# One core, a weight stream split on arrival: moving the release of weights behind each projection's evacuation, one stage per projection in gated attention, and a layer-norm row and the last output block moved

## The chip, the cores and the metric

The kernel runs on one core of a Trainium2 chip. The metric is the time of one execution in device microseconds (us). Engines go by the profile's names: PE is TensorE (PEld its weight load), DVE is VectorE, ACT is ScalarE, POOL is GpSimd, SP is SyncE, which here only issues transfers.

## What is computed

256 tokens of width 1024 pass, in fp32, through two layers with adaptive modulation and then a second block. Cut to what matters:

```python
def first_block(x, c, ctx, c_ctx, w_mod, b_mod, ln_g, ln_b, ...):
    for i in range(2):                                   # layer 0: attention, layer 1: pooling
        sh1, sc1, g1, sh2, sc2, g2 = adaln_params(c, w_mod[i], b_mod[i])
        hx = modulate(x, sh1, sc1)                       # x * (1 + sc1) + sh1
        y = latent_diff_attention(...) if i == 0 else multiscale_pool(hx, pool_w, pool_scale)
        x = layer_norm(ALPHA * x + g1 * y, ln_g[i, 0], ln_b[i, 0])
        x = layer_norm(ALPHA * x + g2 * swiglu(modulate(x, sh2, sc2), w_in[i], w_out[i]),
                       ln_g[i, 1], ln_b[i, 1])

def second_block(x, p, ...):
    u = rms_norm(x, norm_mix) @ w_in
    gq, gk, gv, g_lr, g_r, mq, mk, mv, gate_a, gate_b = jnp.split(u, points, axis=-1)
    o_a = gla_chunked(gq, gk, gv, log_sigmoid(g_lr @ gate_w2 + gate_b) / 16)
    y_a = (rms_norm(o_a, gla_out_norm) * silu(g_r)) @ w_branch_a
    y_b = moba_attention(rms_norm(mq), rms_norm(mk), mv) @ w_branch_b
    x = x + (sigmoid(gate_a) * y_a + sigmoid(gate_b) * y_b) @ w_out
    x = x + square(relu(rms_norm(x, norm_mlp) @ w_up)) @ w_down
    return x + sigmoid(rms_norm(x, norm_ple) @ w_ple_gate) * (p @ w_ple)
```

## The kernel before

The 256 tokens are two tiles of 128 (`t` = 0 and 1). Nearly all the work is projections of both tiles with weights that are used once. A weight arrives as raw blocks of 128x1024 fp32 (512 KB) in the order of a fixed plan (class `Stream`), by transfers that SP issues into 11 buffers. Each block is split: ACT writes a rounded copy `hi` (L285), DVE writes the rest `lo` (L291), into 8 pairs of buffers. A product is then three matmuls, hi with the activations' hi, lo with their hi, hi with their lo (L376 to L378 in `mmN`, L390 and L392 in `mmK`, L403 to L405 in `mmK_tail`), so one projection of one token tile to 512 columns is 24 matmuls over four blocks. In between, the plan holds "m" blocks of modulation weights, each one DVE product with a row `crow` (L269), whose sums become the columns `mc`.

The kernel sets the order of every engine's work by hand: each engine runs its instructions in the order in which the program emits them. `st.get(key)` returns a block's hi and lo, and emits splits up to it where they are not there yet. `st.done(keys)` says that blocks are used up, and at each key emits the next split (a hi on ACT and a lo on DVE, with at most one modulation product) as far as 7 pairs ahead:

```python
        def done(self, *keys):
            for key in keys:
                ...
                self.ndone += 1
                self.pump()
```

So the place of `st.done` in the code is the place in the ACT and DVE queues at which three or four splits stand. The buffers that they write come free while PE is still at work on the blocks, in the order in which it reads them.

PSUM tiles come from three tags, `big`, `mm` and `tr`, with two buffers each. A projection's result (`mm`) is evacuated by ACT or DVE, transposes (`tr`) by both: ACT writes the hi half of the transposed activations (`hh`, `xTh`, `obT`, L425), DVE the lo half (`hl`, `xTl`, L426).

Places that the change touches:

- **FFN** (`ffn`): six chunks of hidden columns. For chunk j, `do_g` and `do_u` make gate and up for both tiles, `fin` the product h on DVE (L969), then the output of chunk j-1 (`o(j-1,0)`, `o(j-1,1)`) is interleaved with the transposes of h (`tr(j,t)`, L981 on PE). A table `mid` has functions that run after the up projections of a chunk. In layer 0's FFN, `mid_gb` at chunk 4 makes columns (`Gc`, `Bc`, `g1p`) from modulation sums, and `mid_gbr` at chunk 5 makes three rows of them (`col_row`: two times four transposes on PE at L774, two copies on ACT at L775).
- **Attention's projections** (`proj`, `qk_evac`, `qk_tr`) of the second block: mq, mk, mv, gq, gk, gv, with the scores and values of the MoBA attention as steps between them. `qk_evac` copies a projection (L1280), sums squares (L1284), and normalises (L418 on DVE, POOL, L1287 on DVE). `qk_tr` transposes (L1294) and scales (L1297).
- **Gated attention** (`g_z` to `g_fin`): 16 projections `seq`, and a list `steps` of functions between them, one or two behind each. `g_kv` (L1482, L1489) makes states, `g_o` (L1495, L1500) uses them.
- **ba, bb, up**: the branch projections and the MLP's up projection, with `st.done` ahead of the evacuation; `down`: the MLP's output, in the same pattern as `o`.

Of the kernel before, what the change touches and what calls it, by code (L numbers as in the profile page):

```python
# [18 lines left out]
P = 128  # L19
# [44 lines left out]
UPM = 8  # L64
F32K = (0, 1, 2, 3, 4)
VM = (1, 1, 1, 1, 0, 0, 0, 0)
EN = (0, 2, 0)

FFN_CHUNKS = [(0, 512), (512, 512), (1024, 512), (1536, 256), (1792, 512), (2304, 512)]
U_COLS = dict(gq=(0, 512), gk=(512, 512), gv0=(1024, 512), gv1=(1536, 512), gr0=(2064, 512), gr1=(2576, 512),  # L70
# [101 lines left out]
def body(ctx: ExitStack, tc: tile.TileContext, wst, prm, cst, cst2, poolp, xT_d, cT_d, x_d, head, lam_d,  # L172
# [769 lines left out]
    def ffn(l, fp, x1_ready, after0, mid1, after1, mid):  # L942
        J = len(FFN_CHUNKS)
        ops_ = None
        hT = {}
        hs = {}

        def gu(j, t, which, ps, mid={}):
            c0, w = FFN_CHUNKS[j]
            n = D * w // (P * BW)  # L950
            lh = xlh(t)
            if is32((which, l, j)):
                lh = lambda k: xf[t, k // 4][:, k % 4]
            mmN(ps[:, :w], lh, mkey((which, l, j), n), width=w, mid=mid)

        def do_g(j, t):
            ps = mmt()
            gu(j, t, "G", ps)
            w = FFN_CHUNKS[j][1]
            h = fp.t([P, 512], f"h{t}", bufs=2)  # L960
            A.activation(h[:, :w], ps[:, :w], AF.Silu)  # L961
            hs[j, t] = h

        def do_u(j, t, mid={}):
            ps = mmt()
            gu(j, t, "U", ps, mid)
            w = FFN_CHUNKS[j][1]
            h = hs[j, t]
            V.tensor_tensor(h[:, :w], h[:, :w], ps[:, :w], op=OP.mult)  # L969

        def fin(j, which):
            c0, w = FFN_CHUNKS[j]
            st.done(*mkey((which, l, j), D * w // (P * BW)))

        def tr(j, t):
            w = FFN_CHUNKS[j][1]
            n = w // P
            h = hs.pop((j, t))
            ps = trt()
            for i in range(n):  # L980
                TE.transpose(ps[:, i * P:(i + 1) * P], h[:, i * P:(i + 1) * P], ident)  # L981
            hh = fp.t([P, 4, P], f"hh{t}", F32R, bufs=2)
            hl = fp.t([P, 4, P], f"hl{t}", F32R, bufs=2)
            pv = ps.rearrange("p (k t) -> p k t", t=P)[:, :n]
            split_evac(pv, hh[:, :n], hl[:, :n])
            hT[j, t] = (hh, hl)

        def o(j, t, done):
            n = FFN_CHUNKS[j][1] // P
            hh, hl = hT.pop((j, t))  # L990
            if j == J - 1:
                keys = [("O", l, j, i) for i in range(n)]
                mmK_tail(halves(ops_[t]), [(hh[:, i], hl[:, i]) for i in range(n)], keys)
                if done:
                    st.done(*keys[:HN[l]])
                    st.hold = True
                    st.done(*keys[HN[l]:])
                return
            for i in range(n):
                mmK(halves(ops_[t]), (hh[:, i], hl[:, i]), ("O", l, j, i), j == 0 and i == 0, False)  # L1000
                if done:
                    st.done(("O", l, j, i))

        for j in range(J):
            if j == 0:
                do_g(0, 0)
                do_u(0, 0, {XR[l]: x1_ready})
                if XR[l] == 8:
                    x1_ready()
                do_g(0, 1)  # L1010
                fin(0, "G")
                do_u(0, 1)
                fin(0, "U")
# [12 lines left out]
            if j < J - 1:
                if j > 0:
                    o(j - 1, 0, False)
                tr(j, 0)
                if j > 0:  # L1030
                    o(j - 1, 1, True)
                    tr(j, 1)
            else:
                tr(j, 0)
                o(j - 1, 0, False)
                tr(j, 1)
                o(j, 0, False)
                if l == 0:
                    for b in range(2):
                        st.prescale(("PW", b))  # L1040
                after0(ops_[0])
                if l == 0:
                    st.hold = True
                o(j - 1, 1, True)
                mid1()
                o(j, 1, True)
                after1(ops_[1])
                if l == 1:
                    st.hold = False
                    st.pump()  # L1050
# [38 lines left out]
    def mid_gb():  # L1089
        nx["gb"] = mod_cols(1, 0, 1)  # L1090
        g1p = cp.t([P, 8], "g1p")
        V.tensor_tensor(g1p, mcol(1, 2), prmc("psc"), op=OP.mult)
        nx["g1p"] = g1p

    def mid_gbr():
        nx["G"], nx["B"] = col_row(nx["gb"][0]), col_row(nx["gb"][1])
        cur["grow"] = col_row(nx["g1p"])
        nx["cols"] = mod_cols(1, 1, 2)

    mrs = {}  # L1100
# [165 lines left out]
        a, b = CST2[n]  # L1266
        return c2d[:, a:b] if b <= o_ else c2[:, a - o_:b - o_]

    def proj(c, t, fin, mid={}):
        ps = mmt()  # L1270
        mmN(ps, xlh(t), mkey((c,), 4), mid=mid)
        if fin:
            st.done(*mkey((c,), 4))
        return ps

    qk_wait = []

# [23 lines left out]
    for i, (c, t) in enumerate(seq):  # L1301
        if i == 2 and MQ == 8:
            rx_t(1, prmc("nmix"))
        ps = proj(c, t, t == 1, {MQ: lambda: rx_t(1, prmc("nmix"))} if i == 1 else {})
        qk_evac(c, t, ps)
# [66 lines left out]
    seq = [(c, t) for c in ("mv0", "mv1", "gq", "gk", "gv0", "gv1") for t in range(2)]  # L1372
    per = -(-len(steps) // 9)
    for i, (c, t) in enumerate(seq):
        ps = proj(c, t, t == 1)
        if c[:2] == "mv":
            A.activation(mv[:, t, 512 * int(c[2]):512 * int(c[2]) + 512], ps, AF.Copy)
        elif c == "gq":
            A.activation(gq[:, t], ps, AF.Copy)
        elif c == "gk":  # L1380
            A.activation(gk[:, t], ps, AF.Copy)
        else:
            A.activation(gv[:, t, 512 * int(c[2]):512 * int(c[2]) + 512], ps, AF.Copy)
# [119 lines left out]
    def g_fin(t):  # L1503
# [5 lines left out]
        for h in range(GH):  # L1509
# [4 lines left out]
    tr_evac(s[1], 1, *obT)  # L1514
    seq = [("gb0", 0), ("gb0", 1), ("gb1", 0), ("gb1", 1), ("bb0", 0), ("bb0", 1), ("bb1", 0), ("bb1", 1),
           ("ga0", 0), ("ga0", 1), ("ga1", 0), ("ga1", 1), ("gr0", 0), ("gr1", 0), ("gr0", 1), ("gr1", 1)]
    steps = [lambda: (g_z(0), g_z(1)), lambda: g_b(0), lambda: g_b(1), lambda: (g_kl(0), g_kl(1)), lambda: g_qk(0), lambda: g_qk(1),
             lambda: g_a(0), lambda: g_a(1), lambda: g_kv(0), lambda: g_kv(1), lambda: (g_o(0, 0), g_o(1, 0)), lambda: g_kv(2),
             lambda: (g_o(0, 1), g_o(1, 1)), lambda: g_kv(3), lambda: (g_o(0, 2), g_o(1, 2)),
             lambda: (g_o(0, 3), g_o(1, 3))]  # L1520

    def oblh(t):
        return lambda k: (obT[0][:, k, t * P:(t + 1) * P], obT[1][:, k, t * P:(t + 1) * P])
# [1 line left out]
    for i, (c, t) in enumerate(seq):  # L1525
# [7 lines left out]
        if c[:2] == "bb":  # L1533
            ps = mmt()
            mmN(ps, oblh(t), mkey(("bb", f), 4))
            if t == 1:
                st.done(*mkey(("bb", f), 4))
            V.scalar_tensor_tensor(tb[t][:, sl], tb[t][:, sl], 1.0, ps, op0=OP.add, op1=OP.mult)
        else:
            ps = proj(c, t, t == 1)  # L1540
            if c[:2] == "gb":
                A.activation(tb[t][:, sl], ps, AF.Tanh, scale=0.5)
            elif c[:2] == "ga":
                A.activation(ta[t][:, sl], ps, AF.Tanh, scale=0.5)
            else:
                e = tmp()
                A.activation(e, ps, AF.Tanh, scale=0.5)
                V.scalar_tensor_tensor(gs[t][:, sl], e, 1.0, ps, op0=OP.add, op1=OP.mult)
                V.tensor_tensor(gs[t][:, sl], gs[t][:, sl], gon[:, sl], op=OP.mult)
        for _ in range(1 + (1 < i < 6)):  # L1550
            if steps:
                steps.pop(0)()
        if (c, t) == ("gr1", 0):
            while steps:
                steps.pop(0)()
            g_fin(0)
    g_fin(1)

# [2 lines left out]
    for i, (f, t) in enumerate([(0, 0), (1, 0), (0, 1), (1, 1)]):  # L1561
# [68 lines left out]
    for j in range(1, J):  # L1630
# [139 lines left out]
```

## Time and profile before

| | |
|---|---|
| three runs, us | 1155.54, 1156.95, 1157.97 (median 1156.95) |
| the profiled execution, us | 1158.82 |
| its span on the core, us | 1156.8 (2.0 less than its time) |
| mean granted TensorE clock | 0.993 |
| PE busy | 1116.0 us, 96% of the span, 5186 instructions |
| DVE busy | 760.6 us, 66% |
| ACT busy | 558.8 us, 48% |
| POOL busy | 22.7 us, 2% |
| moved | 234.62 MB, mean 203 GB/s |

Busy shares count matmuls, ALU and activation work, not register or semaphore instructions. The matmuls' ends are modelled and overlap, so time is best read from start to start. A wait is the idle time of an engine in front of an instruction, with what ended it.

### The profile page before, as it was taken

To read this page: it belongs to the slowest core of one execution; us is meant where nothing else is said; L and a number is where in the kernel's file an instruction comes from. 1 tells how busy PE (TensorE), PEld (TensorE's weight loads), DVE (VectorE), ACT (ScalarE), POOL (GpSimd) and SP (SyncE) were. 2 spreads that over 40 slices of the span, in tenths; PEclk is the share of its full clock that TensorE was granted. 3 is DMA by queue.
4 is the path that set the end of the run, shared out by engine and by line. 5 is a ranking of instruction groups with operands and counts; after the bars stand their busy time and mean duration, and the time that the engine had idled before them with its cause. 6 is when DMAs were issued, how large, how long until landed. Compare 5 with 4: busy or idle time off the path is not lost. (4 is left out here: it accounts for less than half of the span.)

```text
span 1156.8 us, 14163 instructions
## 1 busy us (share of the span) xinstructions
PE 1116.0 (96%) x5186; PEld 881.8 (76%) x5186; DVE 760.6 (66%) x1114; ACT 558.8 (48%) x913; POOL 22.7 (2%) x35
## 2 busy tenths in 40 slices
PE   7999888999999999999999999999999999999998
PEld 3578665678888776888887787886777877888887
DVE  7984967669986875677346765455545785555465
ACT  3452456454444527544444755457235374445353
POOL 0000000000000000000000110000000000000000
PEclk9999989999999999999999999999999999999999
DMA  9972742569997915668563755444344645464611
GB/s 360 351 274 102 273 145 66 196 236 357 354 419 286 336 58 203 218 225 300 170 231 119 241 188 180 146 164 153 102 146 130 216 151 195 166 210 163 206 38 37
DMA packets 65922, 234.62 MB, mean 203 GB/s; under 512 B 7323, under 2 KB 8347, under 8 KB 65852
## 3 DMA queue, kind: packets, MB, share of 16 engines
q1 hardware_dynamic: 64080, 227.97, 55.7%
q10 hardware_dynamic: 1772, 5.74, 1.5%
q8 instruction: 41, 0.67, 0.2%
q14 instruction: 29, 0.24, 0.1%
HBM read 232.63 MB, written 1.05 MB: 202 GB/s over the span
## 5 line engine op out<-in xcount | busy, mean ns | idle before, releaser
L291 DVE TENSOR_TENSOR lo<-raw,hi 128x1024 fp32r<-128x1024 f32 x316 | 375.2, 1220 | 139.8 <-ACT hi L285 136.1
L285 ACT ACTIVATE hi<-raw 128x1024 fp32r<-128x1024 f32 x316 | 322.5, 1056 | 82.9 <-PE mm L378 60.9
L376 PE MATMUL mm<-hi,xTh 128*128 128x512 f32 (+1 forms) x872 | 337.6, 387 | 4.0 <-ACT xTh L425 2.7
L377 PE MATMUL mm<-lo,xTh 128*128 128x512 f32 (+1 forms) x872 | 331.8, 380 | 2.0 <-DVE lo L291 1.3
L378 PE MATMUL mm<-hi,xTl 128*128 128x512 f32 (+1 forms) x872 | 332.2, 381 | 0.6 <-DVE xTl L738 0.4
L376 PEld LDWEIGHTS mm<-hi,xTh 128*128 128x128 f32 x872 | 164.1, 188 | 40.8 <-issue 4.7
L378 PEld LDWEIGHTS mm<-hi,xTl 128*128 128x128 f32 x872 | 164.0, 188 | 34.0 <-DVE xTl L426 1.9
L377 PEld LDWEIGHTS mm<-lo,xTh 128*128 128x128 f32 x872 | 164.2, 188 | 33.5 <-DVE lo L291 3.6
L269 DVE SCALAR_TENSOR_TENSOR raw<-raw,crow 128x1024 f32<-128x1024 f32 x80 | 96.7, 1218 | 0.0
L390 PE MATMUL big<-hi,hh 128*128 128x512 f32 x256 | 80.6, 396 | 0.0
L390 PE MATMUL big<-lo,hh 128*128 128x512 f32 x256 | 79.2, 391 | 0.0
L392 PE MATMUL big<-hi,hl 128*128 128x512 f32 x256 | 79.0, 390 | 0.0
L425 ACT ACTIVATE hh<-tr 128x512 fp32r<-128x512 f32 (+1 forms) x40 | 23.0, 576 | 97.4 <-PE tr L981 54.8
L961 ACT ACTIVATE h<-mm 128x512 f32<-128x512 f32 (+1 forms) x24 | 13.5, 561 | 90.2 <-PE mm L378 90.2
L426 DVE TENSOR_TENSOR hl<-tr,hh 128x512 fp32r<-128x512 f32 (+1 forms) x40 | 26.3, 661 | 46.3 <-ACT hh L425 45.6
L392 PEld LDWEIGHTS big<-hi,hl 128*128 128x128 f32 x256 | 48.1, 188 | 10.4
L390 PEld LDWEIGHTS big<-lo,hh 128*128 128x128 f32 x256 | 48.0, 188 | 10.3
L390 PEld LDWEIGHTS big<-hi,hh 128*128 128x128 f32 x256 | 46.7, 188 | 8.6
L420 POOL TENSOR_TENSOR st<-st,half 128x4 f32<-128x4 f32 (+1 forms) x28 | 21.8, 778 | 1036.8 <-DVE st L418 1023.6
L1596 DVE TENSOR_TENSOR h<-h 128x512 f32<-128x512 f32 x16 | 11.0, 688 | 33.6 <-ACT h L1595 33.5
L1595 ACT ACTIVATE h<-mm 128x512 f32<-128x512 f32 x16 | 9.6, 599 | 38.0 <-PE mm L378 38.0
L667 ACT ACTIVATE p<-big,st 128x512 f32<-128x512 f32 x16 | 11.0, 689 | 31.7 <-DVE st L666 31.7
(316 smaller groups left out, 1261.5 us busy)
## 6 DMA issues: line engine op xcount, KB each, us to landing
raw<-in_dram SPq DMA_DIRECT2D x426, 512.0 KB, 5.0
row<-in_dram ACTq DMA_DIRECT2D x8, 512.0 KB, 6.4
tok<-in_dram SPq DMA_DIRECT2D x8, 256.0 KB, 7.5
xa<-in_dram SPq DMA_DIRECT2D x2, 512.0 KB, 5.7
out_dram<-sg SPq DMA_DIRECT2D x3, 256.0 KB, 2.0
pmat<-in_dram ACTq DMA_DIRECT2D x1, 544.0 KB
crow<-in_dram ACTq DMA_DIRECT2D x1, 512.0 KB, 6.8
out_dram<-sg SPq DMA_DIRECT2D x2, 128.0 KB, 1.7
```

What stands on the lines that cost most here:

```text
L269: V.scalar_tensor_tensor(raw, raw, 1.0, crow, op0=OP.mult, op1=OP.mult, accum_out=mc[l][:, nb:nb + 1])
L285: A.activation(hi, raw, AF.Copy)
L291: V.tensor_tensor(lo, raw, hi.bitcast(F32), op=OP.subtract)
L376: TE.matmul(ps, h, hi[:, sl], start=s, stop=False)
L377: TE.matmul(ps, h, lo[:, sl], start=False, stop=False)
L378: TE.matmul(ps, l, hi[:, sl], start=False, stop=e)
L390: TE.matmul(halves[f], h, w[:, f * 512:(f + 1) * 512], start=first and b == 0, stop=False)
L392: TE.matmul(halves[f], l, hi[:, f * 512:(f + 1) * 512], start=False, stop=last)
L420: G.tensor_tensor(r, v, half_e[:, :w], op=OP.pow)
L425: A.activation(dh, ps, AF.Copy)
L426: V.tensor_tensor(dl, ps, dh.bitcast(F32), op=OP.subtract)
L961: A.activation(h[:, :w], ps[:, :w], AF.Silu)
```

## The change

1. `st.done` moves behind the evacuation, in `proj` (which now gets the evacuation as a function), in bb, ba and up. `st.done` is the call that emits the next splits, so these stand behind the evacuation in ACT's and DVE's queues.
2. Gated attention has one entry of `steps` per projection: `g_b` of both tiles together, `g_kl` of both, `g_qk(0)`, `g_qk(1)`, `g_a` of both, `g_kv(0)`, then for each head `g_o` of both tiles and the next head's `g_kv`.
3. In layer 0's FFN the row of `Gc` is made in `mid_gb` (chunk 4) and the row of `g1p` in a new `late_row` behind `tr(4, 1)`; `mid_gbr` at chunk 5 keeps the row of `Bc`.
4. In both FFNs and in the MLP, the split of the last output block is forced by a `st.get` ahead of the second-last output.
5. `EN`, which sets where a layer norm's second tile stands among the last outputs, is 2 in place of 0 in one entry.

```diff
-EN = (0, 2, 0)
+EN = (0, 2, 2)
...
                     o(j - 1, 1, True)
                     tr(j, 1)
+                if (j, 1) in mid:
+                    mid[j, 1]()
             else:
                 tr(j, 0)
+                st.get(("O", l, j, FFN_CHUNKS[j][1] // P - 1))
                 o(j - 1, 0, False)
...
         nx["g1p"] = g1p
+        nx["G"] = col_row(nx["gb"][0])
+
+    def late_row():
+        cur["grow"] = col_row(nx["g1p"])
 
     def mid_gbr():
-        nx["G"], nx["B"] = col_row(nx["gb"][0]), col_row(nx["gb"][1])
-        cur["grow"] = col_row(nx["g1p"])
+        nx["B"] = col_row(nx["gb"][1])
...
-    ffn(0, ..., {XM: mid_xa, 2: mid_g2c, 3: mid_g2r, 4: mid_gb, 5: mid_gbr})
+    ffn(0, ..., {XM: mid_xa, 2: mid_g2c, 3: mid_g2r, 4: mid_gb, (4, 1): late_row, 5: mid_gbr})
...
-    def proj(c, t, fin, mid={}):
+    def proj(c, t, evac, mid={}):
         ps = mmt()
         mmN(ps, xlh(t), mkey((c,), 4), mid=mid)
-        if fin:
+        evac(ps)
+        if t == 1:
             st.done(*mkey((c,), 4))
-        return ps
...
-    steps = [lambda: (g_z(0), g_z(1)), lambda: g_b(0), lambda: g_b(1), lambda: (g_kl(0), g_kl(1)), lambda: g_qk(0), lambda: g_qk(1),
-             lambda: g_a(0), lambda: g_a(1), lambda: g_kv(0), lambda: g_kv(1), lambda: (g_o(0, 0), g_o(1, 0)), lambda: g_kv(2),
-             lambda: (g_o(0, 1), g_o(1, 1)), lambda: g_kv(3), lambda: (g_o(0, 2), g_o(1, 2)),
-             lambda: (g_o(0, 3), g_o(1, 3))]
+    steps = [lambda: (g_z(0), g_z(1)), lambda: (g_b(0), g_b(1)), lambda: (g_kl(0), g_kl(1)), lambda: g_qk(0),
+             lambda: g_qk(1), lambda: (g_a(0), g_a(1)), lambda: g_kv(0)]
+    for h in range(GH):
+        def head(h=h):
+            g_o(0, h)
+            g_o(1, h)
+            if h < GH - 1:
+                g_kv(h + 1)
+        steps.append(head)
...
+            V.scalar_tensor_tensor(tb[t][:, sl], tb[t][:, sl], 1.0, ps, op0=OP.add, op1=OP.mult)
             if t == 1:
                 st.done(*mkey(("bb", f), 4))
-            V.scalar_tensor_tensor(tb[t][:, sl], tb[t][:, sl], 1.0, ps, op0=OP.add, op1=OP.mult)
...
-        for _ in range(1 + (1 < i < 6)):
-            if steps:
-                steps.pop(0)()
+        for f_ in steps[i:i + 1]:
+            f_()
...
             trm(j, 0)
+            st.get(("DN", j, 3))
             down(j - 1, 0, False)
```

**PE in layer 0's FFN, chunk 4, between the up projection of the second tile and the gate projection of chunk 5.** `big` is the FFN's output, `h0` and `h1` the hidden chunk, `Gc` and `g1p` the columns. Before:

```order
L378 MATMUL mm_696_2979<-hi_680_2920,xTl_6_71 128x512
L390 MATMUL big_504_2040<-hi_684_2929,hh0_656_2798 128x512 x2
L390 MATMUL big_504_2040<-lo_685_2931,hh0_656_2798 128x512 x2
L392 MATMUL big_504_2040<-hi_684_2929,hl0_657_2799 128x512 x2
...
L981 MATMUL tr_718_3063<-cst_7_72,h0_677_2891 128x128 x4
L390 MATMUL big_505_2041<-hi_684_2929,hh1_674_2862 128x512 x2
...
L981 MATMUL tr_729_3102<-cst_7_72,h1_679_2918 128x128 x4
L376 MATMUL mm_732_3111<-hi_691_2944,xTh_5_70 128x512
```

After:

```order
L378 MATMUL mm_696_2979<-hi_680_2920,xTl_6_71 128x512
L774 MATMUL tr_719_3052<-cst_7_72,Gc_714_3042 128x128 x4
L774 MATMUL tr_720_3058<-cst_7_72,Gc_714_3042 128x128 x4
L390 MATMUL big_504_2040<-hi_684_2929,hh0_656_2798 128x512 x2
...
L981 MATMUL tr_721_3076<-cst_7_72,h0_677_2891 128x128 x4
L390 MATMUL big_505_2041<-hi_684_2929,hh1_674_2862 128x512 x2
...
L981 MATMUL tr_732_3115<-cst_7_72,h1_679_2918 128x128 x4
L774 MATMUL tr_736_3125<-cst_7_72,g1p_716_3047 128x128 x4
L774 MATMUL tr_737_3131<-cst_7_72,g1p_716_3047 128x128 x4
L376 MATMUL mm_738_3137<-hi_691_2944,xTh_5_70 128x512
```

The transposes of `Gc` now stand ahead of all output matmuls of chunk 3, those of `g1p` ahead of the gate projection of chunk 5.

**DVE at the same place.** This piece reads the same in both programs but for line and buffer numbers; it shows what stands ahead of `Gc` and behind it. Of the program after:

```order
L969 TENSOR_TENSOR h1_679_2918<-h1_679_2918,mm_696_2979 128x512
L291 TENSOR_TENSOR lo_698_3007<-raw_667_2839,hi_697_3005 128x1024
L269 SCALAR_TENSOR_TENSOR raw_668_2842,mc1_3_68<-raw_668_2842,crow_8_73 128x1024
...
L291 TENSOR_TENSOR lo_710_3034<-raw_686_2933,hi_709_3032 128x1024
L784 SCALAR_TENSOR_TENSOR mcol_713_3040<-mc1_3_68,prm_1_66 128x8
L862 TENSOR_TENSOR Gc_714_3042<-mcol_713_3040,prm_1_66 128x8
...
L426 TENSOR_TENSOR hl0_723_3082<-tr_721_3076,hh0_722_3081 128x512
L291 TENSOR_TENSOR lo_725_3093<-raw_687_2936,hi_724_3091 128x1024
L269 SCALAR_TENSOR_TENSOR raw_690_2942,mc1_3_68<-raw_690_2942,crow_8_73 128x1024
L291 TENSOR_TENSOR lo_729_3108<-raw_693_2948,hi_728_3106 128x1024
L269 SCALAR_TENSOR_TENSOR raw_694_2951,mc1_3_68<-raw_694_2951,crow_8_73 128x1024
L426 TENSOR_TENSOR hl1_734_3121<-tr_732_3115,hh1_733_3120 128x512
```

Behind h1 stand four lo splits with three modulation products between them, and then the columns; between the two `hl` stand two splits and two products.

**DVE behind mk, the last of the MoBA keys' projections.** `mt` is the normalised projection, `kT2` its scaled transpose, `st4` the norm. Before:

```order
L291 TENSOR_TENSOR lo_1272_5668<-raw_1190_5369,hi_1271_5666 128x1024
L291 TENSOR_TENSOR lo_1275_5674<-raw_1193_5375,hi_1274_5672 128x1024
L291 TENSOR_TENSOR lo_1278_5680<-raw_1196_5381,hi_1277_5678 128x1024
L291 TENSOR_TENSOR lo_1281_5686<-raw_1209_5434,hi_1280_5684 128x1024
L418 TENSOR_SCALAR st4_1289_5701<-st4_1284_5692 128x4
L1287 TENSOR_TENSOR mt_1283_5690<-mt_1283_5690,st4_1290_5703 128x512
L1297 TENSOR_SCALAR kT2_1160_5220<-tr_1291_5706,prm_1_66 128x4x128
L1297 TENSOR_SCALAR kT2_1160_5220<-tr_1293_5738,prm_1_66 128x4x128
```

After:

```order
L418 TENSOR_SCALAR st4_1277_5677<-st4_1272_5668 128x4
L1293 TENSOR_TENSOR mt_1271_5666<-mt_1271_5666,st4_1278_5679 128x512
L291 TENSOR_TENSOR lo_1280_5684<-raw_1198_5385,hi_1279_5682 128x1024
L291 TENSOR_TENSOR lo_1283_5690<-raw_1201_5391,hi_1282_5688 128x1024
L291 TENSOR_TENSOR lo_1286_5696<-raw_1204_5397,hi_1285_5694 128x1024
L291 TENSOR_TENSOR lo_1289_5702<-raw_1217_5450,hi_1288_5700 128x1024
L1303 TENSOR_SCALAR kT2_1160_5220<-tr_1291_5706,prm_1_66 128x4x128
L1303 TENSOR_SCALAR kT2_1160_5220<-tr_1293_5738,prm_1_66 128x4x128
```

The four splits have moved from ahead of the norm to between it and the first `kT2`.

## Rows read from the trace of the kernel before

**Rows 1.** The page, section 1: busy time of each engine, share of the span, instructions.

```profile
PE 1116.0 (96%) x5186; PEld 881.8 (76%) x5186; DVE 760.6 (66%) x1114; ACT 558.8 (48%) x913; POOL 22.7 (2%) x35
```

**Rows 2.** The page, section 5: line, operation, count; busy us, mean ns; idle before, releaser.

```profile
L291 DVE TENSOR_TENSOR lo<-raw,hi 128x1024 fp32r<-128x1024 f32 x316 | 375.2, 1220 | 139.8 <-ACT hi L285 136.1
L285 ACT ACTIVATE hi<-raw 128x1024 fp32r<-128x1024 f32 x316 | 322.5, 1056 | 82.9 <-PE mm L378 60.9
```

**Rows 3.** Waits of PE over the span: us in total, times, longest us.

```profile
PE big L404 <- DVE lo L291: 1.8, 3, 0.6
PE mm L376 <- ACT mv L1377: 1.2, 1, 1.2
```

**Rows 4.** Timeline of PE, 363 to 371: start us, us, operation, count, wait.

```profile
364.25 0.39 PE L378 MATMUL mm<-hi,xTl 128*128 128x512 f32 x1
364.47 0.61 PE L390 MATMUL big<-hi,hh 128*128 128x512 f32 x2
...
367.20 0.60 PE L981 MATMUL tr<-cst,h 128*128 128x128 f32 x4
...
370.76 0.48 PE L376 MATMUL mm<-hi,xTh 128*128 128x512 f32 x1
```

**Rows 5.** Timeline of DVE, 364 to 375.5.

```profile
365.28 1.22 DVE L291 TENSOR_TENSOR lo<-raw,hi 128x1024 fp32r<-128x1024 f32 x1
...
372.12 1.22 DVE L291 TENSOR_TENSOR lo<-raw,hi 128x1024 fp32r<-128x1024 f32 x1
...
373.53 0.17 DVE L862 TENSOR_TENSOR Gc<-mcol,prm 128x8 f32<-128x8 f32 x1
```

**Rows 6.** Timeline of PE and DVE in chunk 5, 392 to 410.

```profile
392.64 1.03 PE L774 MATMUL tr<-cst,Gc 128*128 128x128 f32 x8
...
396.60 0.66 PE L981 MATMUL tr<-cst,h 128*128 128x128 f32 x4 [0.20 <-ACT row L775]
...
403.49 0.40 PE L405 MATMUL big<-hi,hl 128*128 128x512 f32 x1
...
402.05 0.68 DVE L426 TENSOR_TENSOR hl<-tr,hh 128x512 fp32r<-128x512 f32 x1
```

**Rows 7.** Timelines of ACT, DVE and PE at mk, 685 to 697.

```profile
689.51 0.60 ACT L1280 ACTIVATE mt<-mm 128x512 f32<-128x512 f32 x1 [0.30 <-PE mm L378]
...
690.91 0.23 ACT L1284 ACTIVATION_READ_ACCUMULATOR jk<-mm 128x1 f32 x1
...
687.87 4.62 DVE L291 TENSOR_TENSOR lo<-raw,hi 128x1024 fp32r<-128x1024 f32 x4
...
693.76 0.69 DVE L1287 TENSOR_TENSOR mt<-mt,st 128x512 f32<-128x512 f32 x1 [1.19 <-POOL st L420]
...
695.23 1.03 PE L1294 MATMUL tr<-cst,mt 128*128 128x128 f32 x8
```

**Rows 8.** Timelines of ACT, DVE and PE behind gv1, 767 to 782.

```profile
771.55 0.60 ACT L1383 ACTIVATE gv<-mm 128x512 f32<-128x512 f32 x1 [0.30 <-PE mm L378]
...
772.68 1.29 DVE L426 TENSOR_TENSOR obT<-tr,obT 128x512 fp32r<-128x512 f32 x2 [0.17 <-ACT obT L425]
...
774.96 1.03 PE L722 MATMUL tr<-cst,s 128*128 128x128 f32 x8
```

**Rows 9.** Timelines of PE, 822 to 826 (gated attention) and 903 to 906 (ba).

```profile
823.41 1.55 PE L1482 MATMUL tr<-gv,gk 64*128 64x256 f32 x6 [1.44 <-DVE gst L1489]
...
905.10 0.50 PE L377 MATMUL mm<-lo,xTh 128*128 128x512 f32 x1 [0.32 <-DVE lo L291]
```

**Rows 10.** Windows: us, busy (count) of PE, PEld, DVE, ACT, POOL; granted clock; DMA share, GB/s.

```profile
823.40:828.00 4.60, 4.59 (x14) 3.09 (x15) 1.86 (x4) 0.00 (x0) 0.00 (x0) 0.63 0.44 167
155.50:160.20 4.70, 1.02 (x5) 0.22 (x4) 4.42 (x12) 1.60 (x7) 1.02 (x1) 0.83 0.66 210
160.20:163.00 2.80, 2.80 (x12) 2.46 (x13) 2.73 (x5) 1.96 (x8) 0.00 (x0) 0.50 0.91 313
436.50:442.30 5.80, 3.57 (x16) 1.90 (x14) 5.08 (x6) 4.98 (x9) 0.54 (x1) 1.00 0.98 375
```

More of the change, by code (lines that the diff above doesn't have):

```diff
@@ L1303, in body @@
             rx_t(1, prmc("nmix"))
[L1304 to L1305 removed]
+        proj(c, t, lambda ps: qk_evac(c, t, ps), {MQ: lambda: rx_t(1, prmc("nmix"))} if i == 1 else {})
         if i >= 2:
@@ L1374, in body @@
     for i, (c, t) in enumerate(seq):
[L1375 to L1383, printed above, removed]
+        dst = dict(mv=mv, gv=gv, gq=gq, gk=gk)[c[:2]][:, t]
+        if c[2:]:
+            dst = dst[:, 512 * int(c[2]):512 * int(c[2]) + 512]
+        proj(c, t, lambda ps: A.activation(dst, ps, AF.Copy))
         while qk_wait:
@@ L1535, in body, with gate @@
             mmN(ps, oblh(t), mkey(("bb", f), 4))
+            V.scalar_tensor_tensor(tb[t][:, sl], tb[t][:, sl], 1.0, ps, op0=OP.add, op1=OP.mult)
             if t == 1:
                 st.done(*mkey(("bb", f), 4))
-            V.scalar_tensor_tensor(tb[t][:, sl], tb[t][:, sl], 1.0, ps, op0=OP.add, op1=OP.mult)
-        else:
[L1540 to L1545, printed above, removed]
+        elif c[:2] != "gr":
+            dst = (tb if c[1] == "b" else ta)[t][:, sl]
+            proj(c, t, lambda ps: A.activation(dst, ps, AF.Tanh, scale=0.5))
+        else:
+            def gate(ps):
                 e = tmp()
@@ L1549, in body @@
                 V.tensor_tensor(gs[t][:, sl], gs[t][:, sl], gon[:, sl], op=OP.mult)
-        for _ in range(1 + (1 < i < 6)):
-            if steps:
-                steps.pop(0)()
+            proj(c, t, gate)
+        for f_ in steps[i:i + 1]:
+            f_()
         if (c, t) == ("gr1", 0):
-            while steps:
-                steps.pop(0)()
             g_fin(0)
@@ L1566, in body @@
         mmN(ps, xlh(t), mkey(("ba", f), 4), mid={BA: lambda: tr_evac(gs[1], 1, xTh, xTl)} if i == 1 else {})
+        V.scalar_tensor_tensor(ta[t][:, sl], ta[t][:, sl], 1.0, ps, op0=OP.add, op1=OP.mult)
+        V.tensor_tensor(ta[t][:, sl], ta[t][:, sl], tb[t][:, sl], op=OP.add)
         if t == 1:
             st.done(*mkey(("ba", f), 4))
-        V.scalar_tensor_tensor(ta[t][:, sl], ta[t][:, sl], 1.0, ps, op0=OP.add, op1=OP.mult)
-        V.tensor_tensor(ta[t][:, sl], ta[t][:, sl], tb[t][:, sl], op=OP.add)
         if i == 2:
@@ L1596, in up @@
         V.tensor_tensor(h, h, h, op=OP.mult)
+        if t == 1:
+            st.done(*mkey(("UP", j), 4))
         hs[j, t] = h
```

4 lines of the change are left out of this document (1 added, 3 removed).

## The prediction, made before the changed kernel ran

> **What bounds the kernel now.** I read the page's busy times first. PE is busy for 96% of the span [rows 1], so there is little to win on PE but its waits, and much to lose: any place where PE is made to wait is new time. The second view is the costliest groups: splits take most of DVE's and ACT's time, 1.22 us for a lo and 1.06 us for a hi [rows 2]; the lo is the slower, so four splits hold DVE for 4.62 us in a row [rows 7]. The third view is PE's waits. Those that this change could remove are small: three of 0.6 us for the lo of a last output block and one of 1.2 us for the evacuation of mv [rows 3], and in gated attention one of 1.44 us [rows 9]. The last view is the timelines around the places that move. They show when DVE, which works off its queue in program order, gets to what PE will now ask for. That is the heart of the case: the change moves nothing out of the kernel (the number of instructions on each engine stays), it only moves what stands ahead of what.
>
> **The Gc row in chunk 4.** Before, PE ends the up projection's matmuls with the one at 364.25, issues the next at 364.47, and goes on with output matmuls that need nothing new [rows 4]. DVE is still behind: from 365.28 to 372.12 it takes six instructions, 1.14 us each, a seventh follows, and Gc is written at 373.53 + 0.17 = 373.70 [rows 5]. Nothing in the change shortens that queue; the splits in it write buffers that PE left long ago. Now the transposes of Gc stand ahead of the output matmuls, so PE waits from 364.47 to 373.70: +9.2 us. The transposes move here from chunk 5; three rows took 392.64 to 396.60 there, 1.3 us each with their small waits [rows 6], so about 0.9 without.
>
> From 374.6 the old order follows. The output for the first token tile took 364.47 to 367.20, and the transposes of h0, the other output and the transposes of h1 took 367.20 to 370.76 [rows 4]: 2.73 and 3.56. So h0's transposes stand at 377.3 and those of h1 end at 380.9. DVE writes hl0 at about 378.8 and then, before hl1, works off two splits and two products: 4 x 1.14 = 4.6 us, so hl1 is written at about 384.1. The g1p row needs both `tr` buffers; its second half needs the one that hl1 frees. That is a wait of about 2.8 us. The gate projection starts at about 384.8 in place of 370.76: **+14.0** (9.2 and 2.8 of waiting, 1.8 to 2.0 of moved transposes).
>
> In chunk 5 two of three rows go, 2 x 1.3 = 2.6 us of PE. But the tail needs hl of the first tile, which DVE writes at 402.05 + 0.68 = 402.73, while PE uses it at 403.49 [rows 6]; DVE is not made faster there, so only 0.76 of the 2.6 us is gained, and the rest becomes a wait for hl. The early `st.get` takes away one wait of 0.6 for lo [rows 3]. Together **-1.4**. Both ends for the FFN: if hl came along with PE, -2.6 - 0.6; if the wait for lo only changes its name, -0.8.
>
> **The other two forced splits** take away the other two waits of 0.6 [rows 3]: **-1.2**; nothing if DVE's time is only pushed to hl. The change of EN swaps one lo with one step of the layer norm; one wait goes and one of the same kind comes: 0, within 0.6 either way [rows 3].
>
> **Splits behind the evacuation at mk.** Before, the four lo of 687.87 to 692.49 run during the projection, ahead of the norm [rows 7]. After, they stand behind the evacuation. ACT copies at 689.51 and has the squares read at 691.14; only then come four hi of 1.06 us, until 695.4. DVE has the norm (with the 1.19 us that it waits for POOL) at about 693.1, and then four lo, 4.62 us, until 697.7. Only then comes kT2, which frees a `tr` buffer at about 698.4. PE's eight transposes stand at 695.23 [rows 7]; the second four, at about 695.6, need that buffer: +2.8. At the three earlier projections of this stage with two tiles the fourth lo is late for the next projection by what the norm and the copy put ahead of it; I take 0.45 each, +1.3, between 0 and one lo each, 3.7. Together **+4.1**.
>
> **MoBA.** The copy of mv no longer waits behind four hi: -1.2 [rows 3]. In return the scores' exponentials and the copies of gk stand behind four hi, up to 4 x 1.06 = 4.2 us [rows 2]; most of it lies beside a projection of 5.5 us (24 matmuls of 0.23 each, as the start of one to the next [rows 4]), so I take +1.7. Together **+0.5**, between -1.2 and +3.0.
>
> **Behind gv1.** ACT copies gv at 771.55 and took obT's hi halves right after it, DVE its lo halves at 772.68 for 1.29 us [rows 8]. Now four hi (until 776.4) and four lo (from 773.2, 4.62 us, until 777.8) stand between them, and obT's lo halves are written at 778.4 and 779.1. PE's eight transposes of the other tile, at 774.96, need both `tr` buffers: the second four move from 775.4 to 779.1, **+3.7**. What hides the splits now is the projection itself; that cover is gone.
>
> **Gated attention.** g_kv(1) no longer follows g_kv(0) directly, so PE's wait of 1.44 us goes [rows 9], and with it the low clock behind it: 823.40 to 828.00 had a granted clock of 0.63 [rows 10], 4.6 x 0.37 = 1.7 us. **-3.1**, between -4.7 and 0 (two g_b together, and the scores' stages, may wait for DVE or ACT instead).
>
> **ba.** There PE already waits 0.32 us for a lo [rows 9]; now four lo stand behind the evacuation, with the norm's wait for POOL in between, about one lo later: **+1.2**, between 0 and 4.6. The MLP's up and down: 0, since PE has a whole projection of time before it needs the next block.
>
> **The clock.** After the stretch of 155.50 to 160.20, in which PE was busy for 1.02 of 4.70 us, the next 2.8 us ran at a granted clock of 0.50 (1.2 of 2.4 GHz); after 436.50 to 442.30, with 3.57 of 5.80 us, it had stayed at 1.00 [rows 10]. The wait of 9.2 us is of the first kind, at a price of 2.8 x 0.5 = 1.4 or somewhat more; those of 2.8 to 3.7 lie between. I take **+2.2**, between 0 and 6. The Trainium skill ("TensorE: Matmul & The Clock Gate", section "HAM oscillation — how this bites in real kernels") says that a long wait between matmuls throttles PE again, so that the work behind it starts cold, each time; by that every one of the four new waits costs what rows 10 show once, 5.6 or more, and the sum would be higher by 3.4. That is a rival below; rows 10 show one case on either side.
>
> **Sum:** 14.0 - 1.4 - 1.2 + 4.1 + 0.5 + 3.7 - 3.1 + 1.2 + 2.2 = **+20.0 us**. The profiled execution took 1158.82 us (its span 1156.8 and 2.0 around it), so it would take 1178.8; that execution lies 1.9 above the median of the runs, so against the median I say 1156.95 + 20.0 = **1177**.
>
> **The rivals.** (a) *Only the Gc row counts.* ACT and DVE are idle for half and a third of the span [rows 1], so late splits may cost nothing where a full projection lies ahead. Then 14.0 - 1.4 - 1.2 - 1.2 - 3.1, and 1.4 for the clock: +8.5, 1165.5. Against it: at mk and gv1 it is the evacuation of transposes that stands behind the splits, not the next weights. (b) *The clock falls behind every new wait:* +3.4 to +6 on the sum, 1180 to 1183. (c) *Faster:* DVE is not late at chunk 4, since PE's wait makes room for it. The point that decides is whether Gc is written by 364.5 in place of 373.7; then the waits for Gc and g1p go, and if the splits are in time at mk, gv1 and ba as well, what is left is -1.4 - 1.2 - 1.2 - 3.1 = -6.9: 1150. For it speaks the 1.2 us at mv, where the order before cost a wait. The Trainium skill ("PSUM — Partial Sum Buffer", section "🎯 Summary: rules for kernel authors") says to evacuate promptly because PSUM is small; by that the change gains wherever a matmul waits for a buffer's evacuation, and the trace agrees at mv alone. Against it: seven DVE instructions of 1.14 us whose inputs are there before Gc's, in a queue that the change leaves as it was [rows 5]. (d) *It does nothing measurable:* the gains in gated attention would have to grow to the size of the Gc wait; nothing shows that.
>
> **How the numbers follow.** The forecast has 0.72, (a) 0.12, (b) 0.10, (c) 0.04, (d) 0.02. A measurement of this kernel can tell some 0.2% (2.3 us) from no change. Faster by more than that is (c), 0.04; within it (d), 0.02; slower all the rest, 0.94. The range goes from 1164, under (a), to 1184, over (b); it takes in the bounds of mk, MoBA, gated attention and ba, which don't all fall on one side.
>
> **What would show it right or wrong.** In the changed kernel's profile: PE's largest new wait is at the transposes of L774 for Gc, some 9 us, followed by a low granted clock; a second one at the g1p row, near 3; the transposes behind mk (once L1294) and those of the s tile behind gv1 (L722) have new waits of 2.5 to 4 for DVE; g_kv(1) has none. The waits for lo at L404 are gone. It is wrong if Gc's transposes wait under 2 us, if the granted clock stays at 1.00 behind them, or if the waits at mk and gv1 don't show.

## The result, and the profile after

The changed kernel takes 1173.81 us (median of four runs, 1172.98 to 1175.08) against 1157.46 for the kernel before (1155.54 to 1158.03): a ratio of 1.0143, with an interval of 1.0131 to 1.0156, or 16.4 us slower. The prediction had been 1177, 20 us slower, in a range of 1164 to 1184. The profiled execution took 1175.08 us with a span of 1173.1.

The page, section 1, shows no new work; the busy times are those of [rows 1] within 5 us, in a span 16 us longer:

```profile
PE 1116.7 (95%) x5186; PEld 883.0 (75%) x5186; DVE 758.4 (65%) x1114; ACT 554.2 (47%) x913; POOL 22.6 (2%) x35
```

So the time went into waits. PE's waits over the span of the changed kernel (engine, line waited for: us in total, times, longest us), to be held against [rows 3]:

```profile
PE tr L774 <- DVE Bc L863: 9.2, 1, 9.2
...
PE mm L377 <- DVE lo L291: 3.4, 3, 1.6
PE tr L722 <- DVE obT L426: 3.3, 1, 3.3
...
PE tr L1300 <- DVE kT L1303: 2.2, 1, 2.2
...
PE big L405 <- DVE hl L426: 1.4, 1, 1.4
PE mm L376 <- ACT gk L1383: 1.3, 1, 1.3
PE tr L1438 <- DVE la L1433: 1.0, 1, 1.0
...
PE tr L774 <- ACT row L775: 0.7, 1, 0.7
```

The three waits at L404, that for mv and that for gst are gone; new ones stand in their place, most of them for DVE. The largest is the one at Gc (the column Bc that the row names is written right behind it). The timeline of PE there, which answers to [rows 4]:

```profile
362.25 0.39 PE L378 MATMUL mm<-hi,xTl 128*128 128x512 f32 x1
...
371.85 1.94 PE L774 MATMUL tr<-cst,Gc 128*128 128x128 f32 x8 [9.21 <-DVE Bc L863]
373.44 1.20 PE L390 MATMUL big<-hi,hh 128*128 128x512 f32 x2
...
376.93 0.60 PE L981 MATMUL tr<-cst,h 128*128 128x128 f32 x4
...
380.14 0.60 PE L981 MATMUL tr<-cst,h 128*128 128x128 f32 x4
...
381.92 0.65 PE L774 MATMUL tr<-cst,g1p 128*128 128x128 f32 x4 [0.74 <-ACT row L775]
382.32 0.48 PE L376 MATMUL mm<-hi,xTh 128*128 128x512 f32 x1
```

and that of DVE, which answers to [rows 5]:

```profile
363.28 1.22 DVE L291 TENSOR_TENSOR lo<-raw,hi 128x1024 fp32r<-128x1024 f32 x1
...
370.12 1.22 DVE L291 TENSOR_TENSOR lo<-raw,hi 128x1024 fp32r<-128x1024 f32 x1
...
371.53 0.17 DVE L862 TENSOR_TENSOR Gc<-mcol,prm 128x8 f32<-128x8 f32 x1
...
378.20 0.69 DVE L426 TENSOR_TENSOR hl<-tr,hh 128x512 fp32r<-128x512 f32 x1 [5.94 <-ACT hh L425]
...
383.71 0.69 DVE L426 TENSOR_TENSOR hl<-tr,hh 128x512 fp32r<-128x512 f32 x1
```

DVE's queue is as long as before: from its first lo to Gc 8.25 us (363.28 to 371.53), before 8.25 (365.28 to 373.53 [rows 5]). Only PE now asks for Gc at the start of that queue. Then the roles turn: DVE sits idle for 5.94 us until PE has caught up. From the last up matmul to the gate projection it is 20.07 us, before 6.51 [rows 4]: +13.56.

The granted clock around this wait (windows, columns as in [rows 10]):

```profile
362.00:371.50 9.50, 0.64 (x3) 0.19 (x1) 8.87 (x14) 1.06 (x1) 0.00 (x0) 0.64 0.99 363
371.50:374.00 2.50, 2.15 (x9) 2.10 (x10) 0.66 (x5) 0.77 (x2) 0.00 (x0) 0.50 1.00 410
374.00:377.00 3.00, 3.00 (x13) 2.37 (x12) 0.00 (x0) 0.42 (x1) 0.00 (x0) 0.86 0.85 347
377.00:380.00 3.00, 3.00 (x17) 2.52 (x16) 1.54 (x2) 2.43 (x3) 0.00 (x0) 1.00 0.00 0
```

The clock fell during the wait and was still at half (1.2 GHz) when PE came back.

Behind mk, the splits stand between the norm and the copy that frees the `tr` buffer, as the order showed. DVE and PE of the changed kernel, for [rows 7]:

```profile
704.89 4.62 DVE L291 TENSOR_TENSOR lo<-raw,hi 128x1024 fp32r<-128x1024 f32 x4
709.43 2.25 DVE L1303 TENSOR_SCALAR kT<-tr,prm 128x512 f32<-128x512 f32 x3
...
710.23 0.66 PE L1300 MATMUL tr<-cst,mt 128*128 128x128 f32 x4 [2.20 <-DVE kT L1303]
```

and behind gv1, for [rows 8]:

```profile
787.85 4.63 DVE L291 TENSOR_TENSOR lo<-raw,hi 128x1024 fp32r<-128x1024 f32 x4 [5.81 <-ACT hi L285]
792.39 1.28 DVE L426 TENSOR_TENSOR obT<-tr,obT 128x512 fp32r<-128x512 f32 x2
...
793.13 1.25 PE L722 MATMUL tr<-cst,s 128*128 128x128 f32 x8 [3.30 <-DVE obT L426]
```

In both, PE's wait ends when DVE has done the copy that now stands behind four lo.

**Where the time went.** The order of the projection matmuls is the same in both programs, so the same matmul can be found in both traces; the difference of its start times, stage by stage, tells what each stage gave. All in us, each rounded by itself; sums below are made before rounding. The clock has its own line, but for the low clock of the kernel before in gated attention, which both columns count with that stage. The 1.4 of chunk 4 is named in two lines and counts once.

| stage | forecast | measured |
|---|---|---|
| Gc and g1p in chunk 4 | +14.0 | +13.6, of which 1.4 clock |
| chunk 5 with its forced split | -1.4 | -1.4 |
| the two other forced splits | -1.2 | -0.8 and -0.5 |
| EN | 0 | -1.0 and +1.0 |
| mq and mk | +4.1 | +1.3 and +2.4 |
| MoBA: mv, gk | +0.5 | -1.5 and +1.7 |
| behind gv1 | +3.7 | +3.7 |
| gated attention | -3.1 | -4.2 |
| ba | +1.2 | +0.9 |
| MLP | 0 | -0.3 |
| low clock (chunk 4, from 453.3 and from 794.7) | +2.2 | 1.4 + 1.6 + 1.6 |
| ahead of the first changed instruction | | -2.0 |

The last line is no effect of the change. In the trace before, the granted clock was 0.50 on a busy stretch from 87.0 to 90.2, where the trace after has 1.00 (86.7 to 89.9), and a low clock behind 160 lasted until 165.4, in the trace after until 163.2.

### The profile page after: what moved, and what is told of

Read it like the earlier page. It is cut to its first block, busy times and chain, and to the rows that moved or that the text cites. A ratio compares the mean times of both kernels' runs of the same rounds, so it can differ in the third digit from the quotient of the medians.

```text
span 1173.1 us, 14129 instructions
## 1 busy us (share of the span) xinstructions
PE 1116.7 (95%) x5186; PEld 883.0 (75%) x5186; DVE 758.4 (65%) x1114; ACT 554.2 (47%) x913; POOL 22.6 (2%) x35
## 4 chain that ended last, share of the span: by engine, by line
PE 75%; DVE 13%; ACT 5%; issue 4%; DMA 2%; POOL 0%; SPq 0%; DVEq 0%; POOLq 0%; ACTq 0%
PE mm L378 15%; PE mm L376 15%; PE mm L377 15%; PE big L390 12%; PE big L392 6%; DVE lo L291 5%; DVE junkb L526 2%; DVE raw L269 2%; DMA raw<-in_dram 1%; PE big L384 1%; ACT hi L285 1%; DVE st L666 1%; PE big L405 1%; PE big L403 1%; PE big L404 1%
## 5 line engine op out<-in xcount | busy, mean ns | idle before, releaser
L285 ACT ACTIVATE hi<-raw 128x1024 fp32r<-128x1024 f32 x316 | 317.7, 1055 | 59.0 <-PE mm L378 35.1
L961 ACT ACTIVATE h<-mm 128x512 f32<-128x512 f32 (+1 forms) x24 | 13.5, 562 | 91.3 <-PE mm L378 91.3
```

The costliest lines, as they stand in the source:

```text
L285: A.activation(hi, raw, AF.Copy)
```

## The experiments

The kernel before ran beside each group of experiments, with medians of 1157.21 (1 to 4), 1156.70 (5, 6 with 19 fillers, 8 and 9) and 1157.67 us (6 with 9 fillers, 7 and 10). The changed kernel has only its own four runs, so a difference from it of under 1 us says nothing.

**1 and 2: the rows of Gc and g1p, taken back and alone.** The edit of 1, in the kernel after; that of 2 is point 3 of the change by itself, in the kernel before:

```diff
-        nx["G"] = col_row(nx["gb"][0])
-
-    def late_row():
+
+    def mid_gbr():
+        nx["G"], nx["B"] = col_row(nx["gb"][0]), col_row(nx["gb"][1])
         cur["grow"] = col_row(nx["g1p"])
-
-    def mid_gbr():
-        nx["B"] = col_row(nx["gb"][1])
...
```

> The changed kernel, with the rows of Gc and g1p made at chunk 5 again. Theory (PE waits 9.2 us for Gc because DVE works off seven splits and products first): that wait, the low clock behind it and the moved transposes go, 13.5 us in the trace, and two rows come back at chunk 5 for about 0.7; so 12.8 us less than the changed kernel, 1161. Rival (most of the loss is the late splits of the projections, and the wait at Gc is partly made up later): 6 us less or fewer, 1168 or more.

Measured: 1162.28 us, 1.0043 (1.0029 to 1.0058) of the kernel before, 11.5 less than the changed kernel.

> The kernel before, with only the rows of Gc and g1p moved to chunk 4. Theory: the wait for Gc stands alone, 12.8 us more than before, 1170. Rival (the wait needs the late release of the other parts as well, or later stages give it back): under 6 us more, below 1163.

Measured: 1170.66 us, 1.0114 (1.0091 to 1.0137), 13.5 more than the 1157.21 of the kernel before in these runs. The rows cost 11.5 us with the rest of the change and 13.5 without it, and the rest costs 5.1. 13.5 and 5.1 are 2.2 more than the whole, which is within the interval of experiment 2 (2.7 us either way). The theory holds, both rivals fall.

**3: release ahead of the evacuation again**, in the kernel after; `proj` for the four places:

```diff
-        evac(ps)
         if t == 1:
             st.done(*mkey((c,), 4))
+        evac(ps)
```

> The changed kernel, with the release of weights ahead of the evacuation again in all four places. Theory (late splits stand in front of the evacuation of transposes): the waits behind mk, mv, gk, gv1 and at ba go back to those of before, 3.7 + 0.2 + 5.2 (with the clock) + 0.9, and the 0.3 of the MLP is lost; about 9.5 us less than the changed kernel, 1164. Rival (the gain of 4.2 us in gated attention comes from the late release, not from the stages): then it is lost as well, about 5 us less, 1169.

Measured: 1165.3 us, 1.0069 (1.0050 to 1.0088), 8.5 less than the changed kernel. In its trace the waits for kT, for obT and for gk are gone and the 1.1 us for mv are back. Gated attention keeps its gain. That is the theory, 1.3 us above the time that it gave. The wait for la is gone as well, but that can't be put down to the release: in experiments 4 and 9, which release ahead of the evacuation there too, it is 0.9 and 1.0. In the trace of this run the clock was low just ahead of it,

```profile
796.70:800.20 3.50, 3.50 (x9) 2.77 (x9) 0.69 (x1) 3.45 (x5) 0.00 (x0) 0.51 0.05 13
```

so PE came to la 1.6 us later than at a clock of 1.00, which is more than the wait.

**4: the stages of gated attention alone**, in the kernel before (the new `steps` and one of them per projection, as in the change).

> The kernel before, with only the new stages of gated attention. Theory (the wait of 1.44 us between two g_kv and the low clock behind it go): 3 to 4.2 us less than before, 1153 to 1154. Rival (that gain needs the late release): no difference from before, within 1 us.

Measured: 1152.78 us, 0.9964 (0.9952 to 0.9976), 4.4 less than the kernel before. The gain belongs to the stages. It is 0.2 us over the upper end of what was expected, and the interval of the runs reaches from 2.8 to 5.6.

**5: both rows behind the transposes of h1**, in the kernel after:

```diff
-        nx["G"] = col_row(nx["gb"][0])
...
     def late_row():
+        nx["G"] = col_row(nx["gb"][0])
         cur["grow"] = col_row(nx["g1p"])
```

> The changed kernel, with the row of Gc made behind the transposes of h1 in chunk 4, next to that of g1p, so 6.3 us of PE's own work later. Theory (the wait is the time from PE's arrival until DVE has written Gc): PE waits some 3 us there in place of 9.2, with no low clock behind it, and the kernel takes 6 to 7.5 us less than the changed one, 1166 to 1168. Rival (what costs is to have the two rows in chunk 4 at all, since their buffers and copies hold up the transposes of h): the wait only moves to another tr tile, within 2 us of the changed kernel, 1172 to 1175.

Measured: 1170.38 us, 1.0128 (1.0102 to 1.0153), 3.4 less than the changed kernel: neither of the two. One of the four runs took 1176.69, so the trace has to tell. PE in its timeline:

```profile
369.30 0.60 PE L981 MATMUL tr<-cst,h 128*128 128x128 f32 x4
373.80 1.12 PE L774 MATMUL tr<-cst,Gc 128*128 128x128 f32 x4 [3.90 <-DVE hl L426]
375.60 1.11 PE L774 MATMUL tr<-cst,Gc 128*128 128x128 f32 x4 [0.69 <-ACT row L775]
377.40 1.11 PE L774 MATMUL tr<-cst,g1p 128*128 128x128 f32 x4 [0.69 <-ACT row L775]
379.20 1.11 PE L774 MATMUL tr<-cst,g1p 128*128 128x128 f32 x4 [0.69 <-ACT row L775]
```

The wait did shrink with PE's later arrival, from 9.2 to 3.9 us. But it now ends with hl0, which stands behind the columns on DVE, and then four halves go one after the other through the one `tr` buffer that is free, 1.8 us each at a low clock, since the other is held until DVE has written hl1. So the theory's first half holds (the wait is arrival against DVE's queue, though another instruction of that queue ends it), and the rival has the rest.

**6: fillers in front of Gc**, in the kernel after, to see what the clock costs:

```diff
         nx["g1p"] = g1p
+        keep(19)
         nx["G"] = col_row(nx["gb"][0])
```

> The changed kernel, with 19 matmuls of 128x512 on data that nobody reads, in front of the transposes of Gc, to keep PE at work while it waits for DVE; at the 0.43 us that one of them took elsewhere in the program before they fill 8.2 of the 9.2 us. Theory (the low clock behind the wait costs 0.7 us at the transposes and 0.8 at the output matmuls): the granted clock stays at 1.00 there and 1.5 us go, 1172.3. Rival (those 1.5 us are not the clock's but the restart of the pipeline and PSUM): no difference, within 0.5 us.

Measured: 1179.2 us, 1.0191 (1.0174 to 1.0208), 5.4 more. The fillers' row:

```profile
361.74 16.47 PE L216 MATMUL tr<-crow 128*128 128x512 f32 x38
```

19 fillers are 38 rows of the trace and took 0.86 us each, not 0.43: I had taken the 0.43 us from one row to the next for the time of an instruction. They overran Gc by some 7 us. The clock was still to be read in this trace: the transposes of Gc took 0.79 us from start to next start (378.05 to 378.84) in place of 1.59, the output of the first tile 2.86 in place of 3.49. So I ran it with 9.

> The changed kernel with 9 filler matmuls in front of the transposes of Gc; one took 0.86 us in the run with 19 (two rows of the trace each), so 9 fill 7.7 of the 9.2 us and end before Gc is written. Theory (the low clock costs 1.4 us there): a granted clock of 1.00 behind the wait and 1.4 us less than the changed kernel, 1172.4, with the first output matmul of chunk 3 0.8 us earlier and the transposes of h0 1.4 us earlier. Rival (the fillers themselves delay the transposes): 0 or more.

Measured: 1172.49 us, 1.0134 (1.0117 to 1.0151), 1.3 less than the changed kernel, which the runs alone can't tell from none. The trace can:

```profile
372.61 1.06 PE L774 MATMUL tr<-cst,Gc 128*128 128x128 f32 x8 [1.48 <-DVE Bc L863]
373.42 0.71 PE L390 MATMUL big<-hi,hh 128*128 128x512 f32 x2
```

with windows of

```profile
371.50:374.00 2.50, 1.40 (x11) 1.34 (x12) 1.41 (x8) 0.74 (x2) 0.00 (x0) 1.00 1.00 390
374.00:377.00 3.00, 3.00 (x17) 2.50 (x16) 0.00 (x0) 0.46 (x2) 0.00 (x0) 1.00 0.98 400
```

With PE kept at work the clock stays at 1.00, and the two stretches behind the wait are 0.78 and 0.65 us shorter (1.59 to 0.81, 3.49 to 2.84): the clock's share in the 13.6 us is 1.4.

**7: a row of a column that is ready**, in the kernel after:

```diff
-        nx["G"] = col_row(nx["gb"][0])
+        nx["G"] = col_row(nx["g2c"])
```

> The changed kernel with the first row made of another column, g2, which was ready two chunks before, in place of Gc: the same transposes and copies at the same place, but nothing to wait for (the layer norm's row G then holds other numbers). Theory (all of the 9.2 us are the wait for DVE's queue, which is as long as before): PE doesn't wait there, and meets DVE's queue later, at the row of g1p, for 2.5 to 3 us, since hl0 stands behind the columns; some 8 us less than the changed kernel, 1165 to 1167. Rival (transposes and row copies in front of the output matmuls cost by themselves): 3 us less or fewer, 1171 or more. Second rival (DVE catches up, no wait at all): 11 us less, 1163.

Measured: 1167.93 us, 1.0096 (1.0074 to 1.0118), 5.9 less than the changed kernel; in the traces the gate projection behind it starts 7.7 us earlier, counted from the last start ahead of the change. PE's first wait in chunk 4 is now

```profile
373.32 0.65 PE L774 MATMUL tr<-cst,g1p 128*128 128x128 f32 x4 [3.00 <-DVE hl L426]
```

The same transposes at the same place cost no wait when the column is there, and PE meets DVE's queue 10 us later, at hl0. That is the theory's picture, with its 3.0 us, and a time 0.9 us above the range that it gave; against the second rival, DVE has not caught up.

**8: release later still**, in the kernel after: that of mq and mk behind `qk_tr`, that of gv1 behind obT of the first tile:

```diff
-        if t == 1:
+        if t == 1 and c != "gv1" and c[:2] not in ("mq", "mk"):
             st.done(*mkey((c,), 4))
...
         if i >= 2:
             qk_tr()
+        if t == 1:
+            st.done(*mkey((c,), 4))
...
     tr_evac(s[0], 0, *obT)
+    st.done(*mkey(("gv1",), 4))
```

> The changed kernel, with the release of the mq and mk blocks behind the transposes and their scaled copy that follow, and that of the gv1 block behind obT of the first tile. Theory (it is the evacuation of transposes that the four splits hold up): the 2.4 us behind mk and the 3.6 us behind gv1, with 1.6 of low clock, go: 6 to 7.5 us less than the changed kernel, 1166.5 to 1168. Rival (the splits have to be done somewhere, and later still means that PE waits for a lo of the next projection): less than 2 us of it is gained, 1172 or more.

Measured: 1169.9 us, 1.0114 (1.0101 to 1.0128), 3.9 less, between what the two gave. Of PE's waits, those for kT and obT are gone, 2.2 and 3.3; in return

```profile
PE mm L377 <- DVE lo L291: 5.8, 6, 1.6
```

are three more waits for lo than the changed kernel has, 2.4 us more. Each is right in part: the copies that free buffers were held up by the splits, and the splits can't be put off freely either.

**9: the parts that gain, composed**, on the kernel before: the stages of gated attention, the two `st.get`, and the late release at mv1 and the MLP's up alone.

```diff
+                st.get(("O", l, j, FFN_CHUNKS[j][1] // P - 1))
...
-        ps = proj(c, t, t == 1)
+        ps = proj(c, t, t == 1 and c != "mv1")
         if c[:2] == "mv":
             A.activation(mv[:, t, 512 * int(c[2]):512 * int(c[2]) + 512], ps, AF.Copy)
+            if t == 1 and c == "mv1":
+                st.done(*mkey((c,), 4))
...
```

> The kernel before, with the parts of the change whose stretch of the trace became shorter: the stages of gated attention, the early split of the last output block, and the late release at mv1 and at the MLP's up alone. Theory (the parts are independent): 4.4 for gated attention as measured alone, 0.75, 0.8 and 0.5 for the splits, 1.3 for mv1, 0.3 for up: 8 us less than before, 1149. Rival (the splits that come later at mv1 are late for gq, and the early splits only delay hl): 4.4 to 5 us less, 1152.5.

Measured: 1147.76 us, 0.9922 (0.9910 to 0.9934), 8.9 less than the 1156.7 of the kernel before in these runs: faster than both kernels. The parts add up to about the 8 us expected: what gated attention gave alone, and what the other stages gave in the pair of traces.

**10: the same, with the two g_b apart.**

```diff
-    steps = [lambda: (g_z(0), g_z(1)), lambda: (g_b(0), g_b(1)), ...
+    steps = [lambda: (g_z(0), g_z(1)), lambda: g_b(0), lambda: g_b(1), ...
```

> The composed kernel of the earlier run at 1147.8, with the two g_b of gated attention behind two projections again, as before. Theory (the wait of 1.0 us for la of the second tile comes from asking for it one projection earlier): the wait goes, 1.0 us less, 1146.8. Rival (the later stages, each now a projection later, wait in its place): no difference.

Measured: 1148.01 us, 0.9923 (0.9907 to 0.9938). The wait for la is gone from the trace, and its last matmuls start 1.9 us earlier than in the run before it, of which 0.7 lie ahead of the edit; the times of the runs show no difference. Inconclusive by the runs.

## Why the prediction was right

*The Gc row* was the largest term, and its working held nearly to the digit: 9.2 us forecast from [rows 4] and [rows 5], 9.21 measured, because DVE's queue ahead of Gc takes as long as before (8.25 us in both traces). Experiment 7 shows it by taking the need away; experiment 5 moved PE's arrival, and the wait fell to 3.9, but hl0 ended it there. Rival (c), in which Gc is there when PE asks, falls with the same row.

*The g1p row*: here a step failed. I wrote that "its second half needs the one that hl1 frees", a wait of 2.8 us. The row at 381.92 shows 0.74 us, for ACT's copy of the first half, 1.8 us before DVE starts hl1 at 383.71: both halves went through the buffer that hl0 had freed. The two `tr` buffers aren't taken strictly in turn, which I had supposed without a row for it. Without the clock's 1.4 us, chunk 4 cost 12.1 in place of 14.0; the 1.9 are this wait, which was 2.06 shorter than forecast.

*Chunk 5*: only 1.4 of the 3.2 us that two rows and a lo wait could have given, since the wait for hl takes their place, 1.42 us at L405 in the waits after: as forecast. *The other forced splits* gave 1.3, forecast 1.2. Neither they nor `EN` were run by themselves; what they gave rests on the pair of traces.

*The late splits* at mk, gv1 and ba: 3.7, 3.7 and 0.9, forecast 4.1, 3.7 and 1.2; at MoBA 0.2 for 0.5. Evacuating ahead of the splits gained 1.5 us at mv, where 1.2 was forecast, and 0.3 at the MLP's up. Experiment 3 takes all of it away at once, 8.5 us; the low clock behind gv1 is gone from its trace, but one as long fell at 796.7. Rival (a), that only the Gc row counts, is refuted by experiment 1: with the rows back, the rest of the change is still 5.1 us slower than before, where (a) would have it faster.

*Gated attention*: -4.2 in the pair of traces and -4.4 alone, forecast -3.1: a term that was mis-sized. I counted the wait of 1.44 us and the low clock, 1.7. Experiment 2, which keeps the old stages, has the same wait with a granted clock of 0.63 behind it (833.6 to 838.2); no trace with the new stages has either. Of the other 1.1 to 1.3 us, 0.5 are shorter waits: that for qkd (0.8 to 0.6) and one of 0.3 at L1428 that is gone. The rest I have not traced to a row. The stalls that I set at nothing do cancel: 0.9 us of waits for the exponentials went, 1.0 for la came.

*The clock*: 4.6 us of low clock fell on busy PE in the changed stretch, forecast 2.2. It fell in all four traces with the wait of 9.2 us (the changed kernel, experiments 2, 3 and 8) and cost 1.4 in the changed kernel (experiment 6). The forecast of 1.4 for it met that by chance: its stretch in [rows 10] ends at 163.0, but the clock of the kernel before stayed low on busy PE behind it,

```profile
163.00:165.40 2.40, 2.40 (x9) 1.17 (x8) 0.58 (x2) 1.79 (x6) 0.00 (x0) 0.50 0.26 104
```

so that the same working gives 5.2 x 0.5 = 2.6. The other two falls can't be put down to the change, see below. Rival (b), a fall behind every wait, doesn't hold as such: the wait of 2.2 us at mk left the clock at 1.00 in the changed kernel (710 to 714), though in experiment 1 it was 0.58 behind the same wait (696 to 700). Of the 20 us, 17.8 were forecast for the stages; they gave 13.2, the low clock gave 4.6, and 2.0 went ahead of the change: 15.8 at the last matmul. So the stages were put 4.6 too high, most of it at g1p and in gated attention. Low clock that can't be put down to the change added 3.1 behind the change's start and took 2.0 off ahead of it in this pair of traces; that part of the agreement is luck.

## What to carry to other kernels

A call that releases a buffer may also be the place at which the next work is put into other engines' queues; then moving it moves work, and what counts is what now stands behind that work, above all copies that free PSUM buffers. To move a dependent step earlier on one engine, read from the trace when its input is written, not when its producer could start: the difference to the asking engine's arrival is the new wait, at Gc to within 0.1 us. Measure the parts of a change alone: this one held 8.9 us of gain (experiment 9) behind some 25 of loss (16.4 + 8.9, if the parts add).

## What was not expected of the hardware

The granted clock can't be told from the waits. The wait of 3.3 us behind gv1 stands in six traces. Three of them are the changed kernel, experiment 1 and experiment 6 with 9 fillers; the granted clock behind it there, in this order (columns as in [rows 10]):

```profile
794.00:798.00 4.00, 4.00 (x14) 3.25 (x13) 2.61 (x4) 1.02 (x2) 0.00 (x0) 0.58 0.93 355
```

```profile
781.00:785.00 4.00, 4.00 (x13) 3.28 (x14) 2.81 (x4) 1.19 (x2) 0.00 (x0) 0.57 0.94 352
```

```profile
789.00:795.00 6.00, 4.20 (x22) 3.49 (x23) 5.27 (x8) 2.67 (x5) 0.00 (x0) 1.00 0.97 337
```

Behind the same wait the clock also fell in experiment 6 with 19 fillers (0.53 from 800.4 to 804.0) and in experiment 7 (0.53 from 785.2 to 788.8), and stayed at 1.00 in experiment 5 (790 to 794): four falls, two at full clock. A wait of 1.82 us ahead of a stretch that the change doesn't touch stands in all thirteen traces. In the kernel before it lies at the end of the stretch of 436.50 to 442.30 that [rows 10] show at a clock of 1.00, and the clock stayed there (1.00 from 443.5 to 447.0). In the changed kernel the same stretch began with

```profile
453.30:456.80 3.50, 3.47 (x8) 2.82 (x9) 2.10 (x3) 3.47 (x6) 0.00 (x0) 0.51 0.97 386
```

and the clock fell there in experiments 3 and 6 (19 fillers) too, and in none of the other ten. The fall in experiment 3 at 796.7 has no PE wait over 0.7 us in the 20 us ahead of it. So two of the changed kernel's three falls, 1.6 us each, come at places where other executions with the same waits kept the full clock. Why is open; no run here tells it.

And the filler, a matmul of 128x512 on plain fp32 tiles, counts as two rows in the trace, 0.43 us apart, so 0.86 us each, while each matmul of a split product (hi or lo, written as fp32r) has one row, 0.23 us from the next.
